# Issuing the products of two 64x64 merge steps in turn, inside the block inverses of a gated-DeltaNet encoder

## The chip, the cores and the metric

The kernel runs on one core of a Trainium2 chip. The metric is the device time of one execution in microseconds (us). The kernel before has a median of 2620.11 us over three timed runs (2618.71 to 2625.42). TensorE (PE) multiplies matrices, with the weight load shown apart as PEld; VectorE (DVE), ScalarE (ACT) and GpSimd (POOL) do elementwise work; SyncE (SP) issues most DMAs. Matrix products leave their results in PSUM, of which the kernel uses eight banks of 128 x 512 float32.

## The reference

The model is an encoder of two layers on 1040 tokens (16 meta tokens and 1024 of input), width 1024. Each layer has a mixer and a SwiGLU network. Half of the mixer is a gated DeltaNet with 4 heads of 128, run in both directions in chunks. For every chunk it solves with a unit triangular matrix:

```python
M = jnp.where(strict, jnp.einsum('bnhid,bnhjd->bnhij', kb, k) * decay_mat, 0.0)
A = M + jnp.eye(CHUNK, dtype=M.dtype)
u = lax.linalg.triangular_solve(A, vb, left_side=True, lower=True, unit_diagonal=True)
w = lax.linalg.triangular_solve(A, kb * jnp.exp(G)[..., None], left_side=True, lower=True,
                                unit_diagonal=True)
...
def step(S, inp):
    u_c, w_c, qd_c, kd_c, a_c, gl_c = inp
    v_new = u_c - jnp.einsum('bhcd,bhde->bhce', w_c, S)
    o = jnp.einsum('bhcd,bhde->bhce', qd_c, S) + jnp.einsum('bhij,bhje->bhie', a_c, v_new)
    S = S * gl_c[..., None, None] + jnp.einsum('bhcd,bhce->bhde', kd_c, v_new)
    return S, o
```

The mixer then projects its two halves back to the model's width, and the SwiGLU network follows:

```python
proj = h @ w_in.astype(h.dtype)
...
mix = jnp.concatenate([o, y_sc], axis=-1)
return mix @ w_out.astype(h.dtype)
```

## The kernel before

The dense products (input projection, output projection, SwiGLU) are made from two-part splits of weights and activations: for each tile of 128 inputs three products, high by high, high by low and low by high (lines 156 to 158). `dense` takes the columns in chunks of 346 to 512 and the inputs in eight tiles of 128, so a chunk of an input projection is 24 products in a row, and one of the output projection's halves is 12. After each chunk it takes one entry from each of three lists of pending work (`jobs`, `jobs2`, `jobs3`) and runs it, which is how the chunked recurrence is prepared between dense chunks.

The kernel uses chunks of 128 tokens in the DeltaNet, so in each layer and direction there are 32 matrices of 128x128 to invert (8 chunks by 4 heads; the 16 meta tokens are done apart). `invert(d)` does that for direction d, in place in the buffer `P_`:

- VectorE first solves the 32x32 blocks on the diagonal by substitution (`substitute`, lines 533 to 544).
- `first` (line 560) and `second` (line 568) merge pairs of 32x32 blocks into 64x64 ones. Both go through two pairs, (0, 1) and (2, 3), and issue for each matrix a product of the one pair and then of the other. `third` (line 578) is a product on one 32x32 block for each matrix.
- `fourth` (line 589) and `fifth` (line 594) merge two 64x64 blocks. F_ is the half of the partitions that holds the block solved first, S_ the other half. `fourth` multiplies with operands on F_ and leaves the result on S_; its eviction by ScalarE (line 590) writes it, negated, over the S_ half of `X64`. `fifth` takes that S_ half, multiplies with operands on S_, leaves the result on F_, and its eviction (line 595) writes the finished block into `P_`.

The 32 matrices are taken by `fourth` and `fifth` in four groups of eight; one product of 64x64x64 for each matrix, in float32. The list that `invert` returns has seven entries: `first`, `second`, `third`, then four steps: `fourth` for groups 0 and 1, `fifth` for 0 and 1, `fourth` for 2 and 3, `fifth` for 2 and 3. Each entry is run after one dense chunk. Inverse d takes its PSUM banks from a pool of two ("f" for direction 0, "b" for direction 1).

The order in which the engines' instructions stand is decided by a scheduler when the program is built: it goes by priorities and by its own estimate of when operands are ready. `low` gives a step's products the priority that the dense products have just reached, so that they stand where the chunk ended; the order in which products are written inside `low` is their order of priority, and one that the scheduler finds not ready is passed over by later ones that are.

In each layer the two inverses stand in the input projection: direction 0's ("the first inverse") during the last of the values' tiles and the first z tiles, direction 1's ("the second inverse") in the z tiles behind that. The recurrence follows (`scan_step`): for each chunk and direction 4 loads into the buffer `rec` (lines 780 to 786), the products of lines 802, 808, 818, 831 and 832, VectorE's lines 805 and 840 and ScalarE's lines 812 and 814. `rec` has the buffer that the second inverse used for `X64`. The recurrence's steps are interleaved with the remaining dense work of the input projection and with the output projection's first half, for which ScalarE and VectorE split the convolution group's rows (lines 899 and 900). The output projection's second half reads the recurrence's results, split at lines 928 and 929.

Of the kernel before, what the change touches and what calls it, by code (L numbers as in the profile page):

```python
# [10 lines left out]
AF = mybir.ActivationFunctionType  # L11
# [31 lines left out]
def trunk(ctx: ExitStack, tc: tile.TileContext, xT, w_in, w_ba, w_out, w_gu, w_dn,  # L43
# [12 lines left out]
    def big(tag, dt=F32):  # L56
        return sb.tile([128, 4, L], dt, tag=tag, name=nm(tag))
# [10 lines left out]
    def bank(tag):  # L68
        return psp.tile([128, 512], F32, tag=tag, bufs={"acc": 3, "a": 1, "f": 2, "b": 2}[tag], name=nm("p" + tag))
# [25 lines left out]
    def at_prio(p):  # L95
        tc.cur_priority = p

    mm = nc.tensor.matmul
    act = nc.scalar.activation
# [179 lines left out]
    for l in range(DEPTH):  # L279
# [257 lines left out]
        def invert(d):  # L537
            P_ = Pv[d]
            W, Xi = subs[d]
            tmp = tmp0[0] if d == 0 else big(Y[0][2])  # L540
            XB = tmp[:, 3, 0:1024].rearrange("p (q c) -> p q c", q=32)

            ZB = W.rearrange("p a b -> p (a b)").rearrange("p (q i) -> p q i", q=32)
            nc.vector.transpose(out=XB.rearrange("p q c -> p c q"), in_=Xi.rearrange("p i c -> p c i"))
            nc.vector.transpose(out=ZB.rearrange("p q i -> p i q"), in_=Xi)
            for b in range(4):
                act(out=P_[B[b], :, B[b]], in_=ZB[B[b]], func=AF.Copy)
            pairs = [(0, 1), (2, 3)] if d == 0 else [(3, 2), (1, 0)]
            QS = tmp[:, 2, 0:1024].rearrange("p (q c) -> p q c", q=32)
            X64 = tmp[:, 0:2, :].rearrange("p a b -> p (a b)")[:, 0:2048].rearrange("p (q c) -> p q c", q=32)  # L550
            halves = [slice(0, 16), slice(16, 32)]

            def fb(c):
                return bank("fb"[d]).rearrange("p (q c) -> p q c", c=c)


            def first():
                for qs in halves:
                    ps = fb(32)
                    low(lambda: [mm(ps[B[s], q - qs.start, :], P_[B[f], q, B[s]], XB[B[f], q, :], start=True, stop=True, skip_group_check=True)  # L560
                                 for q in range(qs.start, qs.stop) for (f, s) in pairs])
                    for (f, s) in pairs:
                        act(out=QS[B[s], qs, :], in_=ps[B[s]], func=AF.Copy, scale=-1.0)

            def second():
                for qs in halves:
                    ps = fb(32)
                    low(lambda: [mm(ps[B[f], q - qs.start, :], QS[B[s], q, :], P_[B[s], q, B[s]], start=True, stop=True, skip_group_check=True)
                                 for q in range(qs.start, qs.stop) for (f, s) in pairs])
                    for (f, s) in pairs:  # L570
                        act(out=P_[B[f], qs, B[s]], in_=ps[B[f]], func=AF.Copy)

            def third():
                f, s = pairs[0]
                fo, so = 32 * (f % 2), 32 * (s % 2)
                for qs in halves:
                    ps = fb(32)
                    low(lambda: [mm(ps[B[s], q - qs.start, :], P_[B[s], q, B[s]], QS[B[s], q, :], start=True, stop=True) for q in range(qs.start, qs.stop)])
                    act(out=X64[B[s], qs, fo:fo + 32], in_=ps[B[s]], func=AF.Copy)
                    nc.vector.tensor_copy(X64[B[f], qs, fo:fo + 32], XB[B[f], qs, :])  # L580
                    nc.vector.tensor_copy(X64[B[s], qs, so:so + 32], XB[B[s], qs, :])
                    nc.vector.memset(X64[B[f], qs, so:so + 32], 0.0)


            F_, S_ = (slice(0, 64), slice(64, 128)) if d == 0 else (slice(64, 128), slice(0, 64))

            def fourth(qh):
                ps = fb(64)
                low(lambda: [mm(ps[S_, q, :], P_[F_, 8 * qh + q, S_], X64[F_, 8 * qh + q, :], start=True, stop=True) for q in range(8)])
                act(out=X64[S_, 8 * qh:8 * qh + 8, :], in_=ps[S_], func=AF.Copy, scale=-1.0)  # L590

            def fifth(qh):
                ps = fb(64)
                low(lambda: [mm(ps[F_, q, :], X64[S_, 8 * qh + q, :], P_[S_, 8 * qh + q, S_], start=True, stop=True) for q in range(8)])
                act(out=P_[F_, 8 * qh:8 * qh + 8, S_], in_=ps[F_], func=AF.Copy)

            return [first, second, third] + [lambda f=f, q=q: [f(q), f(q + 1)] for q in (0, 2) for f in (fourth, fifth)]

        l2s = {}

# [82 lines left out]
        def low(f):  # L683

            here = tc.cur_priority
            at_prio(mmp[0])
            f()
            mmp[0] = tc.cur_priority
            at_prio(here)
# [21 lines left out]
        for i in range(4):  # L711
            t = trow()
            if i == 2:
                jobs2.extend([lambda c=c: chunk_a(c) for c in ca])
            if i == 3:
                jobs3.extend([None] * (2 * l) + invert(0))
            inproj(8 + i, to_row(t))
            v = trow() if i % 2 == 0 else row(Y[1] + "f")
            conv(t, v, P_CV + 3 * (8 + i))
            act(out=v, in_=v, func=AF.Silu)  # L720
            jobs.extend([lambda i=i, v=v, c0=c0: v_store(i, v, c0) for c0 in (0, 1, 5)])
# [25 lines left out]
        for j, q in enumerate((4, 5, 0, 6, 7, 1, 2, 3)):  # L747
            lov[0] = j < 2
            if j == 3:
                jobs3.extend(invert(1))  # L750
            if q < 4:
                y3 = sc_tile(q)
            else:
                z_tile(q - 4)
            if j == 0:
                substitute(1)
# [499 lines left out]
        for f in range(FT):  # L1256
# [21 lines left out]
            ps = {}  # L1278
# [98 lines left out]
        for u, (p, b, m) in enumerate(UNITS):  # L1377
            if b == 1 and p in FIRST:
                dh, z = FIRST[p]
                q = 4 * dh + m  # L1380
# [12 lines left out]
            for j in range(NJ):  # L1393
                ps = bks[m, j]
# [108 lines left out]
```

## Time and profile before

| | |
|---|---|
| timed runs, us | 2618.71, 2620.11, 2625.42 |
| span of the profiled execution, us | 2625.6 |
| mean granted TensorE clock, of full speed | 0.983 |
| the first inverse's 64x64 products, first layer | 246.6 to 265.4 us |
| the second inverse's, first layer | 318.2 to 338.3 us |
| the first inverse's, second layer | 1564.6 to 1583.3 us |
| the second inverse's, second layer | 1640.2 to 1660.3 us |

The profiled execution gives its span, from its first instruction to its last; no further time of that execution is at hand, so its span stands for its own time. It is 5.5 us above the median of the timed runs.

How to read the lines below: a row of a timeline has the start in us, the length in us, the engine, the line of the kernel, the operation, the tile written and the tiles read, the shape, the count of merged instructions, and in brackets the idle time of the engine just before and what ended it. A float32 product shows as two passes, so eight products of line 589 are 16. The ends of products are modelled, so their starts are the firmer numbers. A row of windows has the stretch in us and its length, then busy time and count for PE, PEld, DVE, ACT and POOL, the granted clock, the share of DMA time and GB/s. A row of a line's view has the shortest, median and longest duration in ns, and the first and last start in us. SPq is SyncE's queue, on which DMAs are issued.

### The profile page before, as it was taken

The page shows a single profiled execution, that of the slowest core. Times are in us where ns is not written, and L with a number is a line of the kernel's source. Part 1 is how long each engine was busy: PE and PEld are TensorE (multiplying, and loading weights), DVE is VectorE, ACT ScalarE, POOL GpSimd, SP SyncE. Part 2 cuts the span into 40 slices and gives each one's busy share as a digit, 9 for nine tenths or more (in the row PEclk, how much of TensorE's full clock was granted, in tenths as well). Part 3 has the DMA queues.
Part 4 walks back from the last instruction along what each step waited for, and adds up shares of the span by engine and source line. Part 5 has one row for each costly group of instructions (what it writes and reads, how often), then busy time and mean ns, then how long its engine had stood idle before and what let it go on. Part 6 is the DMA issues. An engine that isn't in the chain of part 4 may idle for free. (4 is left out here: it accounts for less than half of the span.)

```text
span 2625.6 us, 45152 instructions
## 1 busy us (share of the span) xinstructions
PE 2512.3 (96%) x17442; PEld 2292.3 (87%) x17442; DVE 1650.8 (63%) x2481; ACT 1046.0 (40%) x1933; POOL 1105.2 (42%) x838
## 2 busy tenths in 40 slices
PE   8999999998999999989999989999989999998997
PEld 6989999998899999989999878998967778886876
DVE  4678433648766666667656874235688777668656
ACT  5564332435233333434445633324442323333444
POOL 2041212225666666645321212222357666665552
PEclk9999999999999999989999989999999999999999
DMA  3458265524422222763224572545333232248431
GB/s 125 127 179 267 88 196 171 183 66 126 136 97 86 102 81 74 242 203 113 94 88 140 177 249 92 184 157 197 111 128 125 91 108 85 76 140 274 130 111 64
DMA packets 213571, 360.03 MB, mean 137 GB/s; under 512 B 25268, under 2 KB 87676, under 8 KB 213356
## 3 DMA queue, kind: packets, MB, share of 16 engines
q1 hardware_dynamic: 180684, 310.69, 36.1%
q10 hardware_dynamic: 30496, 42.09, 5.1%
q0 software_dynamic: 2176, 4.36, 0.6%
q8 instruction: 137, 2.24, 0.4%
q14 instruction: 78, 0.64, 0.1%
HBM read 266.60 MB, written 90.46 MB: 136 GB/s over the span
## 5 line engine op out<-in xcount | busy, mean ns | idle before, releaser
L130 POOL TENSOR_TENSOR wlo<-raw,whi 128x512 fp32r<-128x512 f32 x132 | 178.3, 1353 | 802.7 <-ACT whi L129 723.0
L156 PE MATMUL pacc<-a,whi 128*128 128x346 f32 (+1 forms) x808 | 265.3, 332 | 11.9 <-ACT whi L129 10.4
L158 PE MATMUL pacc<-a,wlo 128*128 128x346 f32 (+1 forms) x808 | 264.7, 329 | 1.4 <-DVE wlo L130 0.7
L156 PE MATMUL pacc<-b,whi 128*128 128x346 f32 (+2 forms) x672 | 235.7, 351 | 0.4 <-DVE a L730 0.4
L158 PE MATMUL pacc<-b,wlo 128*128 128x346 f32 (+2 forms) x672 | 232.7, 348 | 0.0
L157 PE MATMUL pacc<-a,whi 128*128 128x346 f32 (+1 forms) x688 | 226.9, 330 | 2.6 <-DVE a L900 2.4
L157 PE MATMUL pacc<-b,whi 128*128 128x346 f32 (+2 forms) x580 | 201.2, 347 | 0.4 <-DVE b L900 0.4
L129 ACT ACTIVATE whi<-raw 128x512 fp32r<-128x512 f32 x168 | 105.0, 628 | 240.4 <-PE pacc L157 174.5
L156 PEld LDWEIGHTS pacc<-a,whi 128*128 128x128 f32 x808 | 154.0, 191 | 18.1 <-ACT whi L129 11.5
L1043 POOL TENSOR_TENSOR wlo<-rw,whi 128x512 fp32r<-128x512 f32 x92 | 134.7, 1466 | 72.2 <-ACT whi L1042 70.6
L158 PEld LDWEIGHTS pacc<-a,wlo 128*128 128x128 f32 x808 | 154.2, 191 | 3.3 <-issue 1.5
L157 PEld LDWEIGHTS pacc<-a,whi 128*128 128x128 f32 x688 | 132.0, 192 | 6.1 <-issue 2.7
L156 PEld LDWEIGHTS pacc<-b,whi 128*128 128x128 f32 x672 | 127.2, 189 | 10.8 <-issue 2.3
L158 PEld LDWEIGHTS pacc<-b,wlo 128*128 128x128 f32 x672 | 127.1, 189 | 9.8 <-issue 1.1
L1043 POOL TENSOR_TENSOR a<-rw,a 128x512 fp32r<-128x512 f32 x64 | 104.2, 1629 | 67.8 <-ACT a L1042 67.6
L1043 POOL TENSOR_TENSOR b<-rw,b 128x512 fp32r<-128x512 f32 x64 | 92.0, 1439 | 85.0 <-ACT b L1042 50.9
L157 PEld LDWEIGHTS pacc<-b,whi 128*128 128x128 f32 x580 | 109.8, 189 | 8.2 <-issue 0.8
L1042 ACT ACTIVATE whi<-rw 128x512 fp32r<-128x512 f32 x92 | 57.8, 630 | 144.3 <-DVE rw L1270 84.8
L1271 DVE TENSOR_TENSOR rw<-raw,rw 128x512 f32<-128x512 f32 x44 | 96.2, 2187 | 1.2
L1266 DVE TENSOR_TENSOR rw<-rw,rw 128x512 f32<-128x512 f32 x44 | 66.4, 1510 | 48.1 <-POOL wlo L1043 34.6
L1043 POOL TENSOR_TENSOR wlo<-raw,whi 128x512 fp32r<-128x512 f32 x50 | 77.9, 1562 | 34.3 <-ACT whi L1042 33.2
L1042 ACT ACTIVATE b<-rw 128x512 fp32r<-128x512 f32 x64 | 40.3, 630 | 122.0 <-PE pacc L1061 35.2
(970 smaller groups left out, 8417.8 us busy)
## 6 DMA issues: line engine op xcount, KB each, us to landing
raw<-in_w_in SPq DMA_DIRECT2D x112, 256.0 KB
raw<-in_w_gu SPq DMA_DIRECT2D x104, 256.0 KB
rw<-in_w_gu SPq DMA_DIRECT2D x88, 256.0 KB
rec<-aqd SPq DMA_DIRECT2D x62, 256.0 KB
rec<-vkd SPq DMA_DIRECT2D x61, 256.0 KB
rw<-in_w_dn SPq DMA_DIRECT2D x70, 192.0 KB
raw<-in_w_out SPq DMA_DIRECT2D x48, 256.0 KB
b<-ad SPq DMA_DIRECT2D x45, 260.0 KB
```

What stands on the lines that cost most here:

```text
L129: act(out=hi, in_=raw[:, 0:kk, :], func=AF.Copy)
L130: (tt if lov[0] else ptt)(out=lo, in0=raw[:, 0:kk, :], in1=hi.bitcast(F32), op=ALU.subtract)
L156: mm(ps[:, :n], wh, xh[:, n0:n1], start=(k == 0), stop=False)
L157: mm(ps[:, :n], wh, xl[:, n0:n1], start=False, stop=False)
L158: mm(ps[:, :n], wl, xh[:, n0:n1], start=False, stop=(k == K - 1))
L1042: act(out=hi, in_=src, func=AF.Copy)
L1043: ptt(out=lo, in0=src, in1=hi.bitcast(F32), op=ALU.subtract)
L1266: tt(out=s1t, in0=A21, in1=A22, op=ALU.add)
L1271: tt(out=A21, in0=A11, in1=A21, op=ALU.subtract)
```

## The change

`fourth` and `fifth` are replaced by one function, `merges(a, b)`, which does the work of `fourth` for group a and of `fifth` for group b. It issues a product of the one, then a product of the other, for the eight matrices, into two banks; the two evictions follow. Either group can be absent. The four steps become five: `fourth` for group 0 alone, then `fourth` for group 1 with `fifth` for group 0, and so on to `fifth` for group 3 alone. So the list has eight entries for seven.

```diff
-            def fourth(qh):
-                ps = fb(64)
-                low(lambda: [mm(ps[S_, q, :], P_[F_, 8 * qh + q, S_], X64[F_, 8 * qh + q, :], start=True, stop=True) for q in range(8)])
-                act(out=X64[S_, 8 * qh:8 * qh + 8, :], in_=ps[S_], func=AF.Copy, scale=-1.0)
-
-            def fifth(qh):
-                ps = fb(64)
-                low(lambda: [mm(ps[F_, q, :], X64[S_, 8 * qh + q, :], P_[S_, 8 * qh + q, S_], start=True, stop=True) for q in range(8)])
-                act(out=P_[F_, 8 * qh:8 * qh + 8, S_], in_=ps[F_], func=AF.Copy)
-
-            return [first, second, third] + [lambda f=f, q=q: [f(q), f(q + 1)] for q in (0, 2) for f in (fourth, fifth)]
+            def merges(a, b):
+
+                pa_, pb_ = (fb(64) if q is not None else None for q in (a, b))
+
+                def products():
+                    for q in range(8):
+                        if a is not None:
+                            mm(pa_[S_, q, :], P_[F_, 8 * a + q, S_], X64[F_, 8 * a + q, :], start=True, stop=True)
+                        if b is not None:
+                            mm(pb_[F_, q, :], X64[S_, 8 * b + q, :], P_[S_, 8 * b + q, S_], start=True, stop=True)
+
+                low(products)
+                if a is not None:
+                    act(out=X64[S_, 8 * a:8 * a + 8, :], in_=pa_[S_], func=AF.Copy, scale=-1.0)
+                if b is not None:
+                    act(out=P_[F_, 8 * b:8 * b + 8, S_], in_=pb_[F_], func=AF.Copy)
+
+            steps = [(0, None), (1, 0), (2, 1), (3, 2), (None, 3)]
+            return [first, second, third] + [lambda a=a, b=b: merges(a, b) for a, b in steps]
```

Line numbers in what follows are those of the kernel before.

## The prediction

> **What bounds the kernel now.** I read the page's list of engines and its row of slices first, then the windows around the inverses, then the timelines of single bursts there.
>
> ```profile
> span 2625.6 us, 45152 instructions
> PE 2512.3 (96%) x17442; PEld 2292.3 (87%) x17442; DVE 1650.8 (63%) x2481; ACT 1046.0 (40%) x1933; POOL 1105.2 (42%) x838
> ...
> PE   8999999998999999989999989999989999998997
> ...
> 296.00:342.00 46.00, 46.00 (x638) 43.83 (x637) 3.83 (x8) 15.37 (x25) 11.04 (x8) 1.00 0.30 98
> 505.00:521.00 16.00, 11.12 (x59) 9.93 (x58) 12.70 (x25) 10.22 (x31) 5.12 (x3) 0.79 0.99 364
> 514.00:521.00 7.00, 4.57 (x18) 4.38 (x18) 5.97 (x13) 2.33 (x11) 0.00 (x0) 0.51 1.01 385
> 1786.00:1880.00 94.00, 93.62 (x559) 82.48 (x558) 57.04 (x112) 38.04 (x120) 23.44 (x16) 1.00 0.45 149
> ```
>
> TensorE is the bound: 96% of the span, and in the stretch that holds the whole second inverse of the first layer (296 to 342) all 46.00 us at full clock. There, a microsecond less of TensorE work is a microsecond less of time. The third window is the one that will matter beside it: where the first layer passes from the input projection to the output projection (505 to 521), TensorE is busy 11.12 of 16 us, and in its last 7 us the granted clock is 0.51. I put the loss there at 4.88 idle plus 4.57 x 0.49 = 2.2 from the clock, 7.1 us. The same passage of the second layer (1786 to 1880) is idle for 0.38 us only.
>
> The sum below is made against the span of 2625.6 us; the three timed runs have a median of 2620.11, 5.5 us (0.2%) below it. I carry the difference over to the median.
>
> **What a burst of these products costs.** A float32 product appears in the trace as two passes.
>
> ```profile
> 219.52 2.21 PE L560 MATMUL pf<-b,P 32*32 32x32 f32 x128 [0.87 <-DVE b L544]
> 312.01 2.21 PE L578 MATMUL pb<-b,P 32*32 32x32 f32 x64
> L560 PE MATMUL pf<-b,P x128: 191/191/212, 219.5 to 221.5; 32*32 32x32 f32 x128
> L589 PE MATMUL pb<-b,P x64: 218/218/267, 318.2 to 332.1; 64*64 64x64 f32 x64
> 318.17 2.08 PE L589 MATMUL pb<-b,P 64*64 64x64 f32 x32
> 320.17 0.43 PE L156 MATMUL pacc<-a,whi 128*128 128x346 f32 x1
> ...
> 323.76 0.32 PE L157 MATMUL pacc<-a3f,whi 128*128 128x346 f32 x1
> 323.92 0.32 PE L158 MATMUL pacc<-a,wlo 128*128 128x346 f32 x1
> 324.18 2.07 PE L594 MATMUL pb<-P,b 64*64 64x64 f32 x32
> 326.18 0.43 PE L156 MATMUL pacc<-a,whi 128*128 128x346 f32 x1
> 326.44 0.32 PE L157 MATMUL pacc<-a,whi 128*128 128x346 f32 x1
> ```
>
> One pass alone lasts 0.218 us, 32 of them 2.08: they start (2.08 - 0.218) / 31 = 60.1 ns apart. The 32x32 products give the comparison that I need. Line 578 works on one block of the array throughout: (2.21 - 0.191) / 63 = 32.0 ns a pass. Line 560 is issued for two pairs of blocks in turn, the rows and columns of the one disjoint from those of the other: (2.21 - 0.191) / 127 = 15.9 ns. Same shape, same length of burst, half the spacing. The two merges have the same relation: line 589 goes from rows F_ to columns S_, line 594 from rows S_ to columns F_.
>
> The edges: dense products stand 0.16 us apart (323.76, 323.92). From 324.08, where the next dense one would have started, to 326.18 are 2.10 us, and the first gap behind it is 0.26 for 0.16, together 2.20; 32 passes at 60.1 ns are 1.92. So a burst between dense work costs 0.28 us at its edges.
>
> **The change part by part.** Number of products, their shapes, the evictions and all DMAs stay. Four steps of 16 products become five of 8, 16, 16, 16, 8, and the inverses hand over a dense chunk later. In program order the double steps alternate; in the built order of the changed kernel they do so only in part, because the scheduler issues whatever is ready:
>
> - second inverse, first layer: all three double steps alternate, two of them after a start of two and two products of one kind;
> - second inverse, second layer: all three, after starts of three, two and two;
> - first inverse, second layer: one of three, after a start of three and three;
> - first inverse, first layer: none. The halves of each step stand apart, three times with 128x128 products between them.
>
> I take the alternated pass at 60.1 x 15.9 / 32.0 = 29.9 ns, 30.2 less. A double step alternated throughout saves 31 x 30.2 = 0.94 us. In a start of two and two (8 passes) or three and three (12) I count half of the saving, so 0.12 or 0.18 less. Each inverse that gains a position between dense work pays 0.28.
>
> - second inverse, first layer: 3 x 0.94 - 2 x 0.12 - 0.28 = 2.3 saved;
> - second inverse, second layer: 2.82 - 0.42 - 0.28 = 2.1 saved;
> - first inverse, second layer: 0.94 - 0.18 - 0.28 (six positions for five) = 0.5 saved;
> - first inverse, first layer: four positions as before, three splits by other shapes at 0 to 0.28, say 0.14: 0.4 lost.
>
> Sum: 4.5 us saved. Bounds: an alternated pass no faster than the 15.9 ns of the smaller block (saves 44.2 for 30.2 ns, 7.1 us in all), or no faster than 60.1 (only the edges are left: 3 x 0.28 + 0.4 = 1.3 us lost).
>
> The Trainium skill, page "TensorEngine Tiling (Array Packing)", section "Key Properties", says that a change of tiling mode drains TensorE, while a change of tile within a mode does not. The edges of 0.28 us agree with it. By that rule alone the change, which has more bursts and not fewer, adds 1.3 us.
>
> ```profile
> 319.35 0.59 ACT L590 ACTIVATE b<-pb 64x512 f32<-64x512 f32 x1 [3.80 <-PE pb L589]
> 320.28 0.59 ACT L590 ACTIVATE b<-pb 64x512 f32<-64x512 f32 x1 [0.34 <-PE pb L589]
> 337.11 1.21 PE L594 MATMUL pb<-P,b 64*64 64x64 f32 x18
> 338.39 0.33 SPq L780 DMA_DIRECT2D rec<-vkd  x1
> ```
>
> The evictions I cost at nothing. The second product of a group needs the first's eviction (0.59 us); it now comes one step later, behind a chunk of 24 dense products (320.17 to 324.08, 3.9 us). With that cover gone it would be 0.6 us, at most nine times, 5.4. Both banks of a pool are taken in each double step, as before by two groups.
>
> The moved step: the loads of the recurrence (rec, line 780) go out when the last merge has ended, 338.32 and 338.39. They share a buffer with the inverse. The last merge now stands one chunk later in TensorE's order, so the recurrence starts 3.9 us later against the dense work; SyncE's queue holds weight loads (line 128) behind that wait. Until about 500 us dense work covers this (nines in the row of slices). Then comes the passage at 505.
>
> ```profile
> 510.88 4.65 DVE L929 TENSOR_TENSOR o<-b,o 128x260 fp32r<-128x260 f32 x7
> 515.46 1.23 DVE L900 TENSOR_TENSOR a<-b,a 128x1040 fp32r<-128x1040 f32 x1
> 518.36 1.36 DVE L900 TENSOR_TENSOR a3f<-b,a 128x348 fp32r<-128x348 f32 x3
> 513.31 0.99 PE L818 MATMUL pb<-vv,rec 128*128 128x128 f32 x6 [1.58 <-ACT vv L812]
> 516.74 0.66 PE L157 MATMUL pacc<-a,whi 128*128 128x348 f32 x1 [2.43 <-DVE a L900]
> 492.98 1.12 DVE L805 SCALAR_TENSOR_TENSOR vv<-pb,negE,rec 128x128 f32<-128x128 f32 x4
> ```
>
> Here the built order differs. Line 900's first subtraction moves ahead of the eight of line 929, so the wait of 2.43 us goes. What is late next is line 900's third row, now last: VectorE has 8 x 0.66 + 1.36 + 1.23 = 7.9 us before it, TensorE some 18 dense products (2.9) and a step's 24 passes (six took 0.99, so about 3), which leaves a wait of 2 us. And the last full step's line 802 and 808 have no dense work between them any more: line 805's 1.12 us come to the open. 2.4 out, 3.1 in, with a clock that may not fall: I take 0, and 7.1 us either way as bound, the loss that stands there now.
>
> Forecast: 4.5 us less, 2620.1 - 4.5 = 2615.6 us.
>
> **The rivals.**
>
> *The passage closes.* With the first rows ready early, TensorE no longer idles long enough for the clock to be lowered. For it: the 2.43 us wait loses its cause. Against it: the third row is late in its place. At the most -4.5 - 7.1: 2608.5 us.
>
> *The later recurrence decides (slower).* Its chain has 3.9 us less dense work in front of it at both passages. If none of that is covered, the first pays 3.9 and the lowered clock again (2.2), the second 3.9: +10.0 - 4.5, 2625.6 us. It decides once more than 4.5 us are uncovered. For it: at 505 there is no slack at all. Against it: the second passage is busy for 93.62 of 94 us, and the first half of the output projection, eight tiles of 3 x 12 products at 0.16 us (46 us), doesn't read the recurrence at all.
>
> *The alternation does nothing.* Blocks of 64 could already fill what the turn-taking fills for 32; then only the edges count, 2621.4 us. For it: no row shows blocks of 64 in turn. Against it: lines 560 and 578, where the factor is 2.0. This is what the drain rule of that page gives by itself.
>
> **How the numbers follow.** Forecast 0.60, closing passage 0.17, later recurrence 0.15, no alternation 0.08. About 0.3%, 7.9 us, is what a measurement of this kernel can tell from no change; the three runs lie within 6.7. Faster than 2612.2: most of the closing passage and a tenth of the forecast's own spread (2611 to 2620), 0.25. Slower than 2628.0: the later recurrence where it also stalls weight loads, and what I have not seen in the reordering, 0.14. Within: 0.61. Range 2607 to 2627: from just under the closing passage to just above the later recurrence.
>
> **What would show it.** Right: lines 589 and 594 of the second inverses in double steps of about 1.2 us instead of 2.08; in the first layer's first inverse still 60 ns a pass; the windows around the second inverses shorter by 2 us for the same dense work. The passage at about 505 shows line 929's eight no longer ahead of the first line 900, with idle and clock loss near 7 us in sum. Wrong: double steps still near 2 us (alternation), a passage that loses under 3 or over 11 us (my zero), or idle TensorE before 500 us, which nothing here foresees.

## The result, and the profile after

| | median | range | runs |
|---|---|---|---|
| before | 2617.96 us | 2612.36 to 2625.42 | 22 |
| after | 2611.95 us | 2604.57 to 2619.01 | 22 |

The ratio is 0.9976, with a 95% interval of 0.9967 to 0.9985: 6 us less, between 3.9 and 8.6. The forecast was 4.5 less.

The page of the kernel after, its span and its row for TensorE:

```profile
span 2615.9 us, 45160 instructions
PE 2508.6 (96%) x17442; PEld 2290.1 (88%) x17442; DVE 1656.8 (63%) x2481; ACT 1046.3 (40%) x1933; POOL 1109.8 (42%) x838
```

The same number of products, in 3.7 us less of TensorE's time (2512.3 before). The windows of the forecast, in the kernel after (length, busy time of PE, PEld, DVE, ACT, POOL, then the granted clock, the DMA share, GB/s):

```profile
296.00:342.00 46.00, 46.00 (x652) 43.62 (x651) 5.19 (x10) 15.95 (x25) 12.35 (x9) 1.00 0.29 92
505.00:521.00 16.00, 12.04 (x86) 11.65 (x85) 12.74 (x28) 9.28 (x26) 4.96 (x3) 1.00 0.97 354
514.00:521.00 7.00, 7.00 (x52) 7.00 (x53) 7.00 (x20) 0.65 (x4) 0.00 (x0) 1.00 1.01 383
1786.00:1880.00 94.00, 92.77 (x560) 80.84 (x559) 60.05 (x116) 41.87 (x124) 26.87 (x18) 1.00 0.45 154
```

The first window is as full as before, with 14 more counted in it. TensorE has no idle time there, so the evictions, which the prediction put at nothing, cost nothing in the second inverse. In the passage to the output projection (505 to 521) the loss is 16 - 12.04 = 3.96 us of idle time and nothing from the clock; it was 4.88 and 2.2. The second layer's passage lost 0.38 us before and loses 1.23 now.

Numbers of lines from here on are those of the kernel that is spoken of: after, the fourth product is line 594 (eviction 600), the fifth line 596 (eviction 602), and each line behind them stands 8 higher than before (929 is 937); in the experiments they move by a line or two more (the fifth product of e1 is 597, line 730 is 739 in e5 and 740 in e11).

**The double step.** TensorE's timeline in the second inverse of the first layer, after (start, length, instruction):

```profile
325.52 0.32 PE L157 MATMUL pacc<-a3f,whi 128*128 128x346 f32 x1
325.67 0.32 PE L158 MATMUL pacc<-a,wlo 128*128 128x346 f32 x1
325.93 0.27 PE L594 MATMUL pb<-b,P 64*64 64x64 f32 x1
325.93 0.27 PE L596 MATMUL pb<-P,b 64*64 64x64 f32 x1
326.03 0.22 PE L594 MATMUL pb<-b,P 64*64 64x64 f32 x1
326.04 0.22 PE L596 MATMUL pb<-P,b 64*64 64x64 f32 x1
...
326.85 0.22 PE L594 MATMUL pb<-b,P 64*64 64x64 f32 x1
326.86 0.22 PE L596 MATMUL pb<-P,b 64*64 64x64 f32 x1
327.00 0.43 PE L156 MATMUL pacc<-a,whi 128*128 128x346 f32 x1
```

The 32 passes go in pairs, one of each line. From the first start to the last are 0.93 us for 31 steps, 30.0 ns a pass, where it was 60.1. From the first pass to the next dense product are 1.07 us; before it was 2.00 (324.18 to 326.18 in the prediction's rows).

**By stretches.** A wall-clock window of one profile does not hold the same work as that of another. So the dense products of the projections (lines 156 to 158; 5664 in every kernel here) are counted in the trace, and a stretch goes from the start of one of them to the start of another. s1 and s2 hold the first inverse of the first layer and what follows it, s3 its second inverse, s4 the recurrence and the passage; s5 and s6 are s3 and s4 in the second layer.

```
stretch (dense products)        s1        s2         s3         s4         s5         s6
                          926-1140 1140-1200  1285-1430  1430-2600  4190-4330  4330-5000
before                       55.11     10.97      35.12     264.81      36.83     204.79
before, second profile       54.83     10.98      35.12     264.89      36.83     204.65
after                        54.67     13.62      31.80     263.36      33.68     207.56
after, second profile        54.08     12.08      31.80     263.36      33.68     207.55
e1 halves                    56.78     11.08      34.02     265.11      35.75     207.56
e2 second inverse only       53.36     12.03      31.80     262.58      33.68     207.56
e3 first inverse only        55.05     11.43      35.12     265.65      36.83     204.96
e4 later                     55.43     11.08      34.22     261.86      36.26     207.56
e5 all alternated            51.69     16.21      31.82     262.90      32.22     206.87
e6 the same, lone products   54.92     12.48      32.66     261.03      34.81     206.22
e9 four steps                54.27     13.60      33.27     264.99      34.99     205.08
e10 five and four            57.62     11.12      31.80     261.79      34.99     205.07
e11 copies on GpSimd         51.16     17.17      31.82     262.40      32.22     206.54
```

s3 to s6 agree to 0.2 us between profiles of one kernel; s1 and s2 wander by up to 1.5. Where the recurrence starts later, eight of its products (line 808 before, 0.81 us) move out of s3 into s4 and out of s5 into s6. With these put back, the change saves 35.12 - 0.81 - 31.80 = 2.5 us in s3 and 36.83 - 0.81 - 33.68 = 2.3 in s5; it saves 264.85 + 0.81 - 263.36 = 2.3 in s4 and loses 207.56 - 204.72 - 0.81 = 2.0 in s6. The sum is 5.1, within the interval of the timed result. It leaves out what lies outside s3 to s6, where two profiles of one kernel differ by 4 us in a single stretch (last section).

### The profile page after: what moved, and what is told of

It reads as the page before. It is cut to its first block, busy times and chain, and to the rows that moved or that the text cites. A ratio compares the mean times of both kernels' runs of the same rounds, so it can differ in the third digit from the quotient of the medians.

```text
span 2615.9 us, 45160 instructions
## 1 busy us (share of the span) xinstructions
PE 2508.6 (96%) x17442; PEld 2290.1 (88%) x17442; DVE 1656.8 (63%) x2481; ACT 1046.3 (40%) x1933; POOL 1109.8 (42%) x838
```

## The experiments

Each ratio is to the kernel before, run beside the experiment (its medians were 2619.99 us for e1 to e4, 2621.77 for e5 to e7, 2620.33 for e9 to e11), with a 95% interval.

**e1: the two halves of a step one behind the other.** The five steps stay; only the turn-taking goes.

```diff
                     for q in range(8):
                         if a is not None:
                             mm(pa_[S_, q, :], ...)
+                    for q in range(8):
                         if b is not None:
                             mm(pb_[F_, q, :], ...)
```

> The five steps of the changed kernel, the same products in the same double steps, but the eight of one group first and then the eight of the other, so that no two of different blocks follow each other but once a step. Theory A (the time comes from the turn-taking of the two blocks): the double steps of the second inverses last about 2.08 us again instead of 1.15, and with six of them at 0.93 the kernel is 5.6 us slower than the changed one, about the same as before (ratio 0.999 to 1.002). Theory B (the time comes from the five steps and what they reorder behind them, the passage at 505 us above all): 6 us faster than before, ratio 0.998. Theory C (TensorE starts ready passes of another block from further down its queue): double steps stay near 1.15 us.

Measured: 2618.29 us, ratio to before 0.9993 (0.9982 to 1.0005). That is 0.0017 or 4.5 us behind the change; the two intervals overlap a little, so the stretches decide: s3 and s5 are (34.02 - 31.80) + (35.75 - 33.68) = 4.3 us longer. The gain in the second inverses comes from the turn-taking (theory A), not from the five steps (theory B). Theory C is wrong by its number, but not quite. A double step in this kernel:

```profile
322.40 0.32 PE L158 MATMUL pacc<-a,wlo 128*128 128x346 f32 x1
322.65 0.97 PE L594 MATMUL pb<-b,P 64*64 64x64 f32 x13
323.41 0.27 PE L597 MATMUL pb<-P,b 64*64 64x64 f32 x1
323.46 0.22 PE L594 MATMUL pb<-b,P 64*64 64x64 f32 x1
323.51 0.22 PE L597 MATMUL pb<-P,b 64*64 64x64 f32 x1
323.52 0.22 PE L594 MATMUL pb<-b,P 64*64 64x64 f32 x1
323.57 0.22 PE L597 MATMUL pb<-P,b 64*64 64x64 f32 x1
323.58 0.22 PE L594 MATMUL pb<-b,P 64*64 64x64 f32 x1
323.63 0.92 PE L597 MATMUL pb<-P,b 64*64 64x64 f32 x13
324.48 0.43 PE L156 MATMUL pacc<-a,whi 128*128 128x346 f32 x1
```

Three passes of the second half start among the last three of the first, though they are issued behind them. The first half comes to a stop after 13 passes, six and a half products, so this is not the order in which whole products were built. So TensorE does start passes of a free block early, but only about three passes deep: the step takes 1.83 us from its first pass to the next dense product, between 2.00 and 1.07. One thing in e1 isn't as in the change: its recurrence starts late too, but s4 is 265.11, not 263.36. This is taken up under e9.

**e2 and e3: the change in one direction alone.** In e2 `invert(0)`, in e3 `invert(1)` returns the steps of before.

```diff
+            if d == 0:   # e3: d == 1
+                return [first, second, third] + [lambda f=f, q=q: [f(q), f(q + 1)] for q in (0, 2) for f in (fourth, fifth)]
```

> The change in the second inverse of each layer alone; the first inverse has the four steps of before. Theory A: it holds nearly all of the gain, 2.3 and 2.1 us in the inverses by the forecast's sum and what the passage gives, together 4 to 7 us faster than before (ratio 0.9973 to 0.9985); if the first inverse of the first layer costs the 0.4 us forecast, it is as fast as the whole change. A rival (the first inverses, whose windows read 3.6 us longer in the profile after, lose): 3 us faster than the whole change, 9 us faster than before, 0.9965.

> The change in the first inverse of each layer alone, where the built order alternates one of the six double steps. Theory A: 0.5 us saved and 0.4 us lost, so within 1 us of before (ratio 0.9996 to 1.0004), the passage at 505 us as before with 7 us lost in it. The rival by which the first inverse of the first layer loses: 3 us slower, ratio 1.001.

Measured: e2 2613.90 us, 0.9977 (0.9968 to 0.9987), as fast as the whole change; e3 2621.33 us, 1.0007 (0.9996 to 1.0018). The second inverses hold the gain. The rival's 0.9965 for e2 lies outside its interval. e3 cannot tell the forecast's 0.1 us from a loss of 3 by its time; its stretches s1 and s2, 66.48 in sum, are within 0.7 of before, so nothing there shows a loss.

**e4: the kernel before with the last step one chunk later.**

```diff
-            return [first, second, third] + [lambda f=f, q=q: ...]
+            steps = [lambda f=f, q=q: ...]
+            return [first, second, third] + steps[:3] + [None] + steps[3:]
```

> The kernel before with one empty entry ahead of the last step of each inverse: nothing alternates, and the recurrence starts one dense chunk (3.9 us) later as in the change. Theory A with the passage closing: the passage at 505 us loses about 4 us instead of 7, so the kernel is 3 us faster than before (0.9989). The forecast's zero for the passage: no difference (0.9997 to 1.0003). The rival of the later recurrence: up to 10 us slower (1.004).

Measured: 2615.30 us, 0.9991 (0.9979 to 1.0003), too wide to tell 3 us from none. The stretches do: s4 is 264.85 + 0.81 - 261.86 = 3.8 us shorter, s6 2.0 longer than before once the eight products are put back. Nothing alternates here. So in this kernel the later start of the recurrence alone makes the first passage shorter and the second longer. Of the expectations, the first two had no loss at the second passage, and the third had no gain at the first.

**e9: alternated, without the later start.** Four steps an inverse, of 16 products each.

```diff
-            steps = [(0, None), (1, 0), (2, 1), (3, 2), (None, 3)]
-            return [first, second, third] + [lambda a=a, b=b: merges(a, b) for a, b in steps]
+            steps = [[(0, None), (1, None)], [(2, 0)], [(3, 1)], [(None, 2), (None, 3)]]
+            return [first, second, third] + [lambda s=s: [merges(a, b) for a, b in s] for s in steps]
```

> Four steps an inverse as before, of 16, 16, 16 and 16 products: both first groups' fourth product, group 2's fourth with group 0's fifth in turn, group 3's with group 1's in turn, both last fifths. The recurrence then starts no later than before. Theory A: the second inverses save 2 x 0.93 = 1.9 us each (34.22 us to 32.4 in the first layer's stretch, 8 products of line 808 left out); the second layer's passage takes 84.6 us as before, not 87.5; the first layer's takes 73.5 as before, not 70.9. Sum with the first inverses (hidden in the first layer, 1.9 in the second) 4 to 6 us faster than before, 0.9980. The rival (the lengths of the passages come from chance, not from where the recurrence starts): 87.5 and 70.9 again.

Measured: 2615.17 us, 0.9977 (0.9964 to 0.9990). s3 is 1.85 us shorter than before and s5 1.84, where 2 x 0.93 were expected. s6 is 205.08, within 0.4 of before, and s4 264.99 against 264.85: both passages are back. With e4 this shows from both sides that the later start brings the 2.0 us of s6 and most of the gain in s4; it doesn't always. The windows of the passage from 505 to 521 agree; here e9's and then e3's, where it also starts as before:

```profile
505.00:521.00 16.00, 11.35 (x71) 10.76 (x70) 12.18 (x26) 8.12 (x22) 4.96 (x3) 0.89 0.96 352
```

```profile
505.00:521.00 16.00, 11.78 (x61) 10.48 (x60) 12.66 (x25) 11.19 (x35) 5.02 (x3) 0.76 0.97 353
```

Idle time and clock cost 4.65 + 1.25 = 5.9 us and 4.22 + 2.83 = 7.0, against 4.0 after. The exception at the first passage is e1, where the recurrence starts late:

```profile
505.00:521.00 16.00, 12.86 (x75) 12.38 (x74) 12.24 (x26) 8.73 (x25) 4.96 (x3) 0.79 0.98 366
```

Its idle time is 3.14 us, less than after, but the granted clock is lowered (0.50 from 510 to 516 us), which costs 2.7 more: 5.8 in sum. With the eight products put back, its s4 is 0.5 us shorter than before, where the other late kernels gain 2.3 to 4.6. So the later start takes idle time out of s4 in every kernel here (2.6 to 4.0 us where it is late, 4.2 to 4.9 where it isn't); whether the clock falls there as well isn't settled by it, and what settles it stays open. The exceptions at the second passage are e5, e6 and e11, below, which start late too: from dense product 4340 to 5000 they take 204.01, 204.63 and 203.67 us, where after and e4 take 205.96 for the same work.

**e10: five steps in the first layer, four in the second**, to keep the shorter first passage and be rid of the longer second.

> Five steps in the first layer as in the change, four in the second as in the run beside it: the first passage at 70.9 us and the second at 84.6. Theory A: second layer 2.0 us less lost in the passage, 0.65 us less saved in the second inverse (one double step of 0.93 fewer, one burst's edge of 0.28 fewer), 0.9 more saved in the first: 2.3 us faster than the change, 8 us faster than before, 0.9968. The rival: as the change, 0.9975.

Measured: 2612.60 us, 0.9972 (0.9959 to 0.9984). The stretches come about as expected (s5 and s6 are 240.06 in sum and 241.24 after, 1.2 us less where 2.0 - 0.65 were expected); in time it cannot be told from the change.

**e5 and e6: alternated throughout.** Each product of a double step is held behind the one before it; e5 issues group b's first, e6 group a's.

```diff
+                    prev = None
                     for q in range(8):
                         if b is not None:
-                            mm(pb_[F_, q, :], ...)
+                            prev = after(mm(pb_[F_, q, :], ...), prev)
                         if a is not None:
-                            mm(pa_[S_, q, :], ...)
+                            prev = after(mm(pa_[S_, q, :], ...), prev)
```

> The changed kernel with every product of a double step held behind the one before it, the fifth product's group (whose operands come last) first, so that the built order alternates in all four inverses: 12 double steps against 7 in the change, and 23 bursts against 24. Theory A (a pass alternated costs 29.3 ns for 60, so 0.93 us a double step): 5 x 0.93 + 0.28 = 4.9 us faster than the changed kernel, 9 to 11 us faster than before, ratio 0.9958. The rival (the change's time comes from what it reorders behind the inverses, not from the alternation): as the changed kernel, 0.9976.

> As the run beside it, but with the fourth product's group first, whose first product is ready early: in eleven double steps it is issued a few dense products ahead of the other 15 and stands alone there. 30 bursts against 23. Theory A (0.28 us for each burst's edges): 7 x 0.28 = 2.0 us slower than the run beside it, so 0.9966 against before. The rival (a burst's edges cost nothing of their own): no difference between the two.

Measured: e5 2613.23 us, 0.9969 (0.9957 to 0.9981); e6 2611.62 us, 0.9967 (0.9955 to 0.9980). e6's loss against e5 isn't seen in the time; in s3, which holds two of the lone products (at 329.40 and 335.12 us), it is 32.66 - 31.82 = 0.84 us, 0.42 for each. So a burst's edges do cost time, and a lone product more than the 0.28 that the prediction counts for a burst.

e5 is not the 4.9 us ahead of the change that were expected. In the second layer it gains 241.24 - (32.22 + 206.87) = 2.2 us on the change in s5 and s6, but hardly by alternating: two of these 2.2 us are at the second passage (205.96 - 204.01), where TensorE is idle for 0.05 us and not 1.23. In the first layer, beside the kernel before, it saves about 3.3 us in s1 and pays 5.2 in s2. The waits of TensorE in the stretch from 276 to 292 us (waited for: us in total, times, longest), before, after and in e5:

```profile
PE pacc L156 <- DVE b L730: 0.9, 1, 0.9
```

```profile
PE pacc L156 <- DVE b L738: 2.2, 1, 2.2
```

```profile
PE pacc L156 <- DVE b L739: 4.3, 1, 4.3
```

A dense product waits for its bank, and the bank for an eviction on VectorE. VectorE's timeline in e5:

```profile
277.59 2.21 DVE L544 STREAM_TRANSPOSE b<-x 128x1024 f32<-128x1024 f32 x1
279.69 1.87 DVE L545 STREAM_TRANSPOSE x<-x 128x1024 f32<-128x1024 f32 x1
281.60 0.42 DVE L580 COPY b<-b 32x512 f32<-32x512 f32 x1
...
283.35 0.94 DVE L739 TENSOR_TENSOR b<-pacc,b 128x346 f32<-128x346 f32 x2
```

The eviction stands behind the transposes that end the second direction's substitution and behind four copies. VectorE is busy 20.0 of the 22 us from 262 to 284 (20.6 before). TensorE coming there 3 us sooner only waits 3.4 longer, and then the granted clock falls, to 0.50 from 284 to 288 us.

**e11: e5 with the four copies on GpSimd** in the second direction.

```diff
-                    nc.vector.tensor_copy(X64[B[f], ...], ...)
+                    eng = nc.vector if d == 0 else nc.gpsimd
+                    eng.tensor_copy(X64[B[f], ...], ...)
```

> The fully alternated kernel (23 bursts), with the four copies of 0.42 us behind the transposes of the second direction on GpSimd instead of VectorE. It tests where the gain of the first layer's first inverse went. Theory A: VectorE's queue holds the eviction of line 730 behind two transposes and four copies; without the copies the eviction comes 1.7 us earlier and the gap in TensorE at about 284 us falls from 4.61 to 2.9 us, in the fully alternated kernel. The rival (the gap is a late load or ScalarE): it stays at 4.6. In time 1.7 us, 0.9962 against before.

Measured: 2610.54 us, 0.9962 (0.9949 to 0.9975), the fastest here, beside e5's 0.9969 not to be told apart. TensorE's waits in its profile, and two rows of ScalarE:

```profile
283.96 4.26 ACT L547 ACTIVATE P<-x 32x1024 f32<-32x1024 f32 x4 [14.90 <-DVE x L545]
284.33 0.43 PE L156 MATMUL pacc<-a,whi 128*128 128x346 f32 x1 [2.40 <-DVE b L740]
...
288.24 1.15 ACT L129 ACTIVATE whi<-raw 128x512 fp32r<-128x512 f32 x2
288.93 0.43 PE L156 MATMUL pacc<-a,whi 128*128 128x348 f32 x1 [2.25 <-ACT whi L129]
```

The first gap falls from 4.61 to 2.73 us between starts, as expected, so the eviction's place in VectorE's queue is what TensorE waits for. But a second opens behind it, for the high half of the next weights (line 129), which stands on ScalarE behind four copies of 4.26 us in sum (line 547) that themselves follow line 545. s2 is 17.17 us, not shorter than e5's 16.21. The time's agreement with the expectation is therefore no proof of it.

**e7 and e8: both kernels once more.**

> The changed kernel unaltered, beside the two others on one chip. Theory A: 0.9970 to 0.9982 again, and the passage at 505 us without a lowered clock, with about 4 us idle. If the passage's gain was chance in the profiled execution: the clock falls there again in this one, with about 7 us lost.

> The kernel before unaltered, for a second profile of the passage at 505 us. Theory A: about 5 us idle and 2 us from a granted clock near 0.5 there, as in the first profile. If the passage wanders from execution to execution by as much as the change seemed to give there (3 us), this profile shows 4 us lost or less.

Measured: after 2614.46 us, 0.9972 (0.9957 to 0.9986); before, one run of 2623.73 us. The two profiles of each kernel agree in s3 to s6 of the table, so what the passages show is no chance of one execution.

## Why the prediction was right

**The edges and the alternated pass: right in mechanism and size.** Forecast 29.9 ns from the smaller block, measured 30.0. The second inverses save 2.5 and 2.3 us for the 2.3 and 2.1 of the sum, and e1 shows that it is the turn-taking that saves it. The two groups of a double step also write two banks in turn, and no run parts that from the two blocks; the products of line 560 take turns within one bank, and their factor is the same 2.0. The small surplus is about what I took off for the starts of two and two. The built order of the double step from 331.04 is two of line 594, then two of 596, but passes of both start together, at 331.04 and 331.05, which fits e1's look-ahead of three passes. The edges agree with the drain rule of the Trainium skill (page "TensorEngine Tiling (Array Packing)", section "Key Properties"), with 0.42 us for each lone product in e6; the rival that it gave by itself, 2621.4 us, is refuted.

**The first inverses: not resolved.** In the first layer the halves stay apart, as forecast:

```profile
251.01 1.14 PE L596 MATMUL pf<-P,b 64*64 64x64 f32 x16
253.17 1.14 PE L594 MATMUL pf<-b,P 64*64 64x64 f32 x16
257.79 1.14 PE L596 MATMUL pf<-P,b 64*64 64x64 f32 x16
```

(1.14 - 0.22) / 15 = 61 ns a pass. The forecast's 0.4 lost here and 0.5 saved in the second layer are smaller than what s1, s2 and the second layer's stretch (dense products 3914 to 4085, last section) wander.

**The first passage: the step that failed.** The prediction took 0 for the passage at 505 us, with idle time and clock near 7 us in sum as its sign. It gained 2.3 us, and the sum is 4.0. The order moved as foreseen (line 929's eight no longer stand ahead of the first line 900), but not what was late. Rows of the passage after, from several engines (in brackets the idle time before and what ended it):

```profile
507.18 1.05 PE L810 MATMUL pb<-S,b 128*128 128x128 f32 x8
509.15 0.69 DVE L867 TENSOR_TENSOR b3f<-pb,b3f 128x512 f32<-128x512 f32 x1 [1.25 <-DMA b3f<-od]
509.76 1.11 DVE L813 SCALAR_TENSOR_TENSOR vv<-pb,negE,rec 128x128 f32<-128x128 f32 x4
510.16 1.00 PE L816 MATMUL pb<-vv,P 128*128 128x128 f32 x6 [1.92 <-DVE vv L813]
510.34 2.41 POOL L908 TENSOR_TENSOR a<-b,a 128x1040 fp32r<-128x1040 f32 x1 [0.66 <-ACT a L907]
510.80 3.05 DVE L908 TENSOR_TENSOR a<-b,a 128x1040 fp32r<-128x1040 f32 x1
513.90 0.42 PE L157 MATMUL pacc<-a,whi 128*128 128x348 f32 x1 [2.04 <-DVE a L908]
```

I had line 900's third row (908 here) as late, with a wait of 2 us; TensorE waits for none of it. It waits for the recurrence's step (816), since VectorE holds line 813 behind line 867, which waits 1.25 us for a load, and then for the row of line 908 that VectorE makes first. (The sum behind the 2 us was loose besides: by its own row, six passes in 0.99 us, a step's 24 passes take 4 us and not 3, which leaves a wait of 1.) Two waits of 2 us each, with work between them: the clock isn't lowered as it was around 514 before, which is 2.2 of the 3.1 us by which this window's loss fell. That the clock stays up because the idle time is split doesn't hold: in e1 it is split too, into waits of 2.1 and 1.0 us, and the clock falls. The gain of 2.3 us is what these two orders of work gave, in two profiles each; it doesn't follow from the later start alone.

**The later recurrence: a rival that happened in part.** It was given 0.15, with up to 3.9 us at the second passage, and set aside because TensorE is busy for 93.62 of 94 us there. It cost 2.0 us at just that place (and next to nothing in e5 and e11). A stretch without idle time is not a stretch with room: in the new order the eight of line 816 stand right before products that need a copy which ScalarE has not made. Before and after, the waits around it:

```profile
1811.86 0.50 PE L157 MATMUL pacc<-b,whi 128*128 128x512 f32 x1 [0.38 <-DVE b L900]
```

```profile
1801.63 0.96 PE L156 MATMUL pacc<-b,whi 128*128 128x512 f32 x3 [0.69 <-ACT b L907]
1803.62 0.50 PE L157 MATMUL pacc<-b,whi 128*128 128x512 f32 x1 [0.42 <-DVE b L908]
```

0.69 + 0.42 - 0.38 = 0.73 us of the 2.0 are these waits; where the rest lies wasn't followed further.

The total came out within 1.5 us of the forecast because the two errors, 2.3 gained and 2.0 lost, cancel by the stretches. That part of the agreement is luck. The prediction also said that idle time before 500 us would count against it: the wait at 284 us did grow, from 0.86 to 2.25, and s2 is 2.6 and 1.1 us longer than before in the two profiles. e5 and e11 show its mechanism.

## What to carry to other kernels

Products that use disjoint row and column blocks of the array were worth issuing in turn here even in bursts of 2 us: the factor is 2.0 for blocks of 64 as for those of 32, so that it could be read ahead from a pair in the same profile that already took turns. Before spending it, look for the next queue to hold the stretch: here a faster first inverse only reached an eviction sooner that stood behind transposes on VectorE. A busy engine says nothing about slack: a step moved by one chunk cost 2.0 us at the second passage and gained 2.3 at the first, and in other orders of the same work one or the other was gone.

## What the runs showed of the hardware

Three things were not expected. TensorE starts float32 passes of a free block ahead of some three others that were issued first (e1).

VectorE can be held by GpSimd for a whole instruction. In the kernel after, line 533 takes 0.32 us at this size for the first direction (at 239.29 us), but for the second:

```profile
274.00 2.47 POOL L734 TENSOR_TENSOR b<-b,rstd 128x1040 f32<-128x1040 f32 x1 [0.70 <-DVE b L295]
274.20 2.44 DVE L533 TENSOR_TENSOR Tm<-x,x 128x156 f32<-128x156 f32 x1
276.68 0.32 DVE L535 TENSOR_TENSOR x<-x,Tm 128x156 f32<-128x156 f32 x1
```

The long one ends 0.17 us after GpSimd's does. The 3.05 us of line 908 at 510.80, 1.23 before, are the same: GpSimd's ends at 512.75, and 1.23 later is 513.98, for 513.85. The Trainium skill (page "SBUF — State Buffer", section "Who interferes with whom") says that an operation with two SBUF inputs on VectorE blocks against one on GpSimd that reads SBUF, for the whole instruction; these rows agree. The 1.8 us come ahead of the second wait at the first passage.

And one kernel's profiles differ by the clock. From 1546 to 1562 us, after in its second profile and then in its first:

```profile
1546.00:1562.00 16.00, 14.93 (x98) 12.09 (x98) 10.65 (x25) 3.18 (x7) 1.33 (x1) 0.56 0.67 228
```

```profile
1546.00:1562.00 16.00, 14.82 (x141) 12.67 (x142) 12.96 (x30) 5.71 (x9) 2.74 (x2) 0.85 0.80 262
```

The same work (dense products 3914 to 4085, the second layer's first inverse) took 46.54 and 42.66 us. No time in them is idle. The difference of 3.9 us is about two thirds of the whole change, which is why single spans settle nothing here and the stretches do. Before takes 46.66 and 46.97 us for these products and e4 46.90; all other experiments take 41.1 to 44.6. Whether the change itself shortens this stretch isn't shown.
